# One 88-entry phase table for the S5 scan in a two-layer hybrid inference kernel

## The chip, the cores and the metric

The kernel runs on one core of a Trainium2 chip. The metric is the device time of one execution in microseconds (us). Three timed runs of the kernel before are given, and one more execution was taken with the profiler; every row of the trace is from that one.

## The reference, cut to what matters

The program is one inference step of a two-layer backbone with 128 context tokens and 512 latent tokens, 640 in all. Each layer has three token mixers (differential attention, gated linear attention called GLA, and a bidirectional S5 state-space scan), a gated merge, an output projection and a SwiGLU feed-forward network (FFN). The change concerns the S5 scan alone:

```python
def s5_scan(u, lam_re, lam_im, log_dt, b_re, b_im, c_re, c_im, h0, reverse):
    dt = jnp.exp(log_dt)[:, None]
    mag = jnp.exp(lr * dt)
    ar = mag * jnp.cos(li * dt)
    ai = mag * jnp.sin(li * dt)
...
    pr, pim, hr, hi = lax.associative_scan(complex_affine_combine, (a_r, a_i, bu_r, bu_i), axis=1, reverse=reverse)
    hr = pr * h0r - pim * h0i + hr
    hi = pr * h0i + pim * h0r + hi
    y = einsum('gip,blgp->blgi', c_re, hr) - einsum('gip,blgp->blgi', c_im, hi)
```

It runs forward and backward over 32 channel groups of 16 channels, with 64 complex states per group.

## The kernel before

**The S5 scan.** Tokens are taken in chunks of 8, which gives 16 context chunks, 64 latent chunks and a gap column. The first 64 partitions hold the states of the forward direction and the other 64 those of the backward direction. Eight blocks e of four groups each are worked one after the other. Within a block, `s5_pre` projects the input into the chunk states dS (82 columns per group), turns each column back by the phase of its chunk (function `rot`, lines 818 to 821), runs a real-valued decaying scan on VectorE, and turns the columns forward again with a second `rot`. The phases come from a table PH of 2 x 4 x 82 numbers per partition.

**The tables.** `s5_tables` makes, for one layer, what these blocks need: powers PA of the decay, powers E1 (0 to 8) and E8 of the phase of a chunk, and then per block a row buffer R that holds the projection W (1024 numbers), PH and the output table Vc (1280 numbers). R is written out to DRAM as R_d by a DMA on GpSimd's queue (L447), and a second small result Z as Z_d (L459). `s5_load` later reads W and PH back (L779, L780). R has two buffers. The scratch tile tp_ of the phase product has one buffer, and that is the buffer of Z: the first product into tp_ of a block waits until Z_d of the block before has been written. `cmul` (lines 334 to 340) is a complex product of six VectorE instructions, two of which write the scratch.

**PH before.** The two directions have their latent segment at different columns, so each half of the partitions gets a product of its own: 64 entries at column 17 for the forward half, at column 0 for the backward half. ScalarE then copies the 65th entry from a tile E64 (L479) and copies the first 17 entries into the context segment (L480). That is twelve VectorE instructions of 64 partitions x 256 elements and eight ScalarE copies per block.

**Order.** [...] The tables of layer 0 are built at the start of the program, between the modulation, the first norm, the input projection of the S5 branch and the first gate projections. `GLA_FILL` lists which table blocks (T) and gate projections (e) are written where; all of layer 0's blocks are done before the GLA mixer opens. The tables of layer 1 are built inside layer 0's FFN, one block at each "t" of `FFN_FILL`. Every dense projection needs VectorE too: the weights are split into a high part whi on ScalarE (L90) and a low part wlo on VectorE (L201) before TensorE multiplies (L232).

Of the kernel before, what the change touches and what calls it, by code (L numbers as in the profile page):

```python
# [10 lines left out]
F32 = mybir.dt.float32  # L11
# [4 lines left out]
ALU = mybir.AluOpType  # L16
# [4 lines left out]
P = 128  # L21
# [23 lines left out]
    a="AAAAAAAA",  # L45
    s="AAAAAAADAAAAAAADAAAAAAAAAAADADAAAAAAAADADAADAAAAAAAAADAAAAAAAAAADADAAAAAADAADAAAAAAAAADAAA"
       "AAAAAAAADADAAAAAADDDAAAAAAAAAAADAAAAADDAAAAAAAAAAAAAAA",
    r="AADAAAADAAAAAADADAAADAAAAADAAAAADAAADAAAAADAADAD",
# [5 lines left out]
    g="AAAAAAAADAAAAAAA")  # L54
# [8 lines left out]
EPS = 1e-6  # L63
NCH = T // 8
SP_ = 82
RV = 1024 + 8 * SP_
RW = RV + 1280
VEC = dict(n1g=(0, 8), n2g=(8, 8), bmod=(16, 48), qn=(64, 1), kn=(65, 1), sub=(66, 1),
           on=(67, 1), ba=(68, 4), s5d=(72, 4), bglu=(76, 8))
# [7 lines left out]
def tile_hybrid(ctx: ExitStack, tc: tile.TileContext, i: dict, o: dict):  # L77
# [264 lines left out]
    def s5_tables(l, tb, tabs):  # L342
# [54 lines left out]
        for _ in range(3):  # L397
            dve.tensor_mul(t1, co, co)
            dve.tensor_mul(t2, si, si)
            dve.tensor_mul(si, co, si)  # L400
            dve.tensor_scalar_mul(si, si, 2.0)
            dve.tensor_sub(co, t1, t2)
        def bc(ap, n):
            return ap.to_broadcast([P, 32, n])

# [7 lines left out]
        def powers(name, n, r, i_):  # L413
            X = tb.tile([P, 2, 32, n], F32, tag=name, name=f"{name}_{l}", bufs=1)
            pool.memset(X[:, 0, :, 0:1], 1.0)
            pool.memset(X[:, 1, :, 0:1], 0.0)
            dve.tensor_copy(X[:, 0, :, 1], r)
            dve.tensor_copy(X[:, 1, :, 1], i_)
            double(X, 1)
            double(X, 2)  # L420
            double(X, 4, min(4, n - 5))
            return X

        PA = powers("PA", 9, Ar, Ai)
        E1 = powers("E1", 9, co, si)
        E8 = powers("E8", 8, E1[:, 0, :, 8], E1[:, 1, :, 8])
        E64 = tb.tile([P, 2, 32], F32, tag="E64", name=f"E64_{l}", bufs=1)
        cmul(E64[:, 0], E64[:, 1], E8[:, 0, :, 7], E8[:, 1, :, 7], E8[:, 0, :, 1], E8[:, 1, :, 1], tt[:, :, 0], dve, dve)
        PP = tb.tile([P, 2, 32, 10], F32, tag="PP", name=f"PP_{l}", bufs=1)
        pool.memset(PP, 0.0)  # L430
        PW = tb.tile([P, 2, 32, 8], F32, tag="PW", name=f"PW_{l}", bufs=1)
# [29 lines left out]
        for e in range(8):  # L461
            gs = slice(e * 4, e * 4 + 4)
            R = tb.tile([P, RW], F32, tag="R", name=f"R{l}_{e}", bufs=2)
            PH = R[:, 1024:RV].rearrange("p (a b c) -> p a b c", a=2, b=4)
            Vc = R[:, RV:].rearrange("p (g r x o) -> p g r x o", g=4, r=2, o=16)
            tp_ = tb.tile([P, 4, 8, 8], F32, tag="Z", name=f"tp{l}_{e}", bufs=1)
            for rows, w0, w1 in ((slice(0, 64), 17, 0), (slice(64, P), 0, 65)):
                def o64(j):
                    return PH[rows, j, :, w0:w0 + 64].rearrange("p g (a b) -> p g a b", a=8)

                def e1(j):
                    return E1[rows, j, gs, 0:8].unsqueeze(2).to_broadcast([64, 4, 8, 8])

                def e8(j):
                    return E8[rows, j, gs].unsqueeze(3).to_broadcast([64, 4, 8, 8])

                cmul(o64(0), o64(1), e8(0), e8(1), e1(0), e1(1), tp_[rows], dve, dve)
                for j in range(2):
                    act.copy(PH[rows, j, :, w0 + 64:w0 + 65], E64[rows, j, gs].unsqueeze(2))  # L479
                    act.copy(PH[rows, j, :, w1:w1 + 17], PH[rows, j, :, w0:w0 + 17])  # L480
            bcr = bc8[:, e]
            FBt = tb.tile([P, 2, 4, 32], F32, tag="FB", name=f"FB{l}_{e}", bufs=2)
            pool.memset(FBt[:, :, :, 16:32], 0.0)
            FB = FBt[:, :, :, 0:16]
            tm = tb.tile([P, 4, 10, 16], F32, tag="tm", name=f"tm{l}_{e}", bufs=2)
            tf = tm[:, :, 0, :]

            def fb(j):
                return f[:, j * 32 + e * 4:j * 32 + e * 4 + 4].unsqueeze(2).to_broadcast([P, 4, 16])

            cmul(FB[:, 0], FB[:, 1], bcr[:, 0], bcr[:, 1], fb(0), fb(1), tf, dve, dve)
            Wc = tb.tile([P, 4, 2, 8, 16], F32, tag="Wc", name=f"Wc{l}_{e}", bufs=2)

            def pw(t, n):
                return t.unsqueeze(3).to_broadcast([P, 4, n, 16])

            def mid(t, n):
                return t.unsqueeze(2).to_broadcast([P, 4, n, 16])

            cmul(Wc[:, :, 0], Wc[:, :, 1], pw(PW[:, 0, gs], 8), pw(PW[:, 1, gs], 8),  # L500
                 mid(FB[:, 0], 8), mid(FB[:, 1], 8), tm[:, :, 0:8], dve, dve)
            cr, ci = mid(bcr[:, 2], 10), mid(bcr[:, 3], 10)
            tv = tb.tile([P, 4, 10, 16], F32, tag="tm", name=f"tv{l}_{e}", bufs=2)
            dve.tensor_mul(Vc[:, :, 0], cr, pw(PP[:, 0, gs], 10))
            dve.tensor_mul(tv, ci, pw(PP[:, 1, gs], 10))
            dve.tensor_sub(Vc[:, :, 0], Vc[:, :, 0], tv)
            dve.tensor_mul(Vc[:, :, 1], cr, pw(PP[:, 1, gs], 10))
            dve.tensor_mul(tv, ci, pw(PP[:, 0, gs], 10))
            v1 = Vc[:, :, 1].rearrange("p g x o -> p g (x o)")
            dve.scalar_tensor_tensor(v1, v1, -1.0, tv.rearrange("p g x o -> p g (x o)"), op0=ALU.mult, op1=ALU.subtract)  # L510
            cur = (e, R, Wc, FBt, Vc)
            if l == 0:
                tail(*cur)
            elif e:
                tail(*pend)
            pend = cur
            yield
# [256 lines left out]
    subg_of = {}  # L774

    def s5_load(l, e, spa, tabs):
        PH = spa.tile([P, 2, 4, SP_], F32, tag="s_PH", name=f"PH{l}_{e}", bufs=2)
        W = spa.tile([P, 4, 2, P], F32, tag="s_W", name=f"W{l}_{e}", bufs=2)
        sync.dma_start(W.rearrange("p a b c -> p (a b c)"), tabs[0][e, :, 0:1024])  # L779
        sync.dma_start(PH.rearrange("p a b c -> p (a b c)"), tabs[0][e, :, 1024:RV])  # L780
        return W, PH

# [7 lines left out]
    def s5_pre(l, e, sp, r8, RM, ut, s0, fs):  # L790
        gs = slice(e * 4, e * 4 + 4)
        u = ut[e // 4][:, (e % 4) * 4:(e % 4) * 4 + 4, :]
        W, PH = RM

        def tU(role, name, bufs=2):
            return sp.tile([P, 2, 4, SP_], F32, tag="s_" + role, name=f"{name}{l}_{e}", bufs=bufs)

        DEC = sp.tile([P, 4, SP_], F32, tag="s_DEC", name=f"DEC{l}_{e}", bufs=2)
        dve.tensor_mul(DEC, dmask.unsqueeze(1).to_broadcast([P, 4, SP_]),
                        r8[:, e * 4:e * 4 + 4].unsqueeze(2).to_broadcast([P, 4, SP_]))  # L800
        pd = ps_m(f"pds{l}_{e}")
        for g in range(4):
            for ri in range(2):
                pe.matmul(pd[:, ri, g * 81:(g + 1) * 81], W[:, g, ri, :], u[:, g, :], start=True, stop=True)  # L804
        pdv = pd[:, :, 0:324].rearrange("p r (g n) -> p r g n", g=4)
        dS = tU("dS", "dS")
        copy("D", "A", dS[0:64, :, :, 1:17], pdv[0:64, :, :, 0:16])
        copy("D", "A", dS[0:64, :, :, 18:82], pdv[0:64, :, :, 17:81])
        copy("D", "A", dS[64:P, :, :, 81:65:-1], pdv[64:P, :, :, 0:16])
        copy("D", "A", dS[64:P, :, :, 64:0:-1], pdv[64:P, :, :, 17:81])  # L810
        pool.memset(dS[0:64, :, :, 0:1], 0.0)
        pool.memset(dS[64:P, :, :, 65:66], 0.0)
        pool.tensor_copy(dS[0:64, :, :, 17:18], s0[0:64, :, gs].unsqueeze(3))
        pool.tensor_copy(dS[64:P, :, :, 0:1], s0[64:P, :, gs].unsqueeze(3))
        P1, P2, H = tU("P1", "P1", 1), tU("P2", "P2", 1), tU("H", "H")

        def rot():
            fv = "p r g n -> p r (g n)"
            for j, Pj in ((0, P1), (1, P2)):
                dve.tensor_mul(Pj.rearrange(fv), dS.rearrange(fv),  # L820
                               PH[:, j:j + 1].rearrange(fv).to_broadcast([P, 2, 4 * SP_]))

        rot()
        dve.tensor_add(P1[:, 0], P1[:, 0], P2[:, 1])
        dve.tensor_sub(P1[:, 1], P1[:, 1], P2[:, 0])
        fl = "p g n -> p (g n)"
        for ri in range(2):
            dve.tensor_tensor_scan(dS[:, ri].rearrange(fl), DEC.rearrange(fl), P1[:, ri].rearrange(fl), 0.0, ALU.mult, ALU.add)
        rot()
        lo, hi = slice(0, 64), slice(64, P)  # L830
        for ri, op in ((0, dve.tensor_sub), (1, dve.tensor_add)):
            op(H[lo, ri], P1[lo, ri], P2[lo, 1 - ri])
            op(H[hi, ri, :, 80::-1], P1[hi, ri, :, 0:81], P2[hi, 1 - ri, :, 0:81])
            op(fs[hi, ri, gs].unsqueeze(2), P1[hi, ri, :, 81:82], P2[hi, 1 - ri, :, 81:82])
        pool.tensor_copy(fs[lo, :, gs].unsqueeze(3), H[lo, :, :, 16:17])
        return u, H
# [554 lines left out]
```

## Time and profile before

| | |
|---|---|
| timed runs | 2743.64, 2752.35, 2761.11 us (median 2752.35) |
| profiled execution | 2768.95 us |
| its span, first to last instruction | 2767.2 us |
| mean granted TensorE clock | 0.957 of full speed |
| TensorE, VectorE, ScalarE busy | 2608.2, 1683.7, 869.3 us |

Busy times are of the whole span. The tables take a small part of it, in two stretches: about 10 to 180 us (layer 0) and about 990 to 1395 us (layer 1). In the profile DVE is VectorE, ACT is ScalarE, PE is TensorE, POOL is GpSimd and SP the queue that issues loads.

### The profile page before, as it was taken

How to read it: one execution, taken by the hardware profiler on the slowest of the kernel's cores; microseconds unless marked ns; L12 is line 12 of the kernel's file. 1: busy time of each engine (PE TensorE's matmuls, PEld its weight loads, DVE VectorE, ACT ScalarE, POOL GpSimd, SP SyncE). 2: the span in 40 equal slices, each digit the busy share in tenths (PEclk: the TensorE clock that was granted, in tenths of full speed). 3: DMA queues.
4: the chain of work that ended last, by engine and by line, in shares of the span. 5: the costliest groups of instructions: out<-in, count | busy, mean ns of one | idle time of the engine just before them, and what ended most of it. 6: DMA issues, size and time to landing. Idle time of an engine off the chain costs nothing.

```text
span 2767.2 us, 45251 instructions
## 1 busy us (share of the span) xinstructions
PE 2608.2 (94%) x18528; PEld 2445.5 (88%) x18528; DVE 1683.7 (61%) x3784; ACT 869.3 (31%) x1617; POOL 71.6 (3%) x194
## 2 busy tenths in 40 slices
PE   5859989999999999989999799999999999999999
PEld 3748869988999989879999698899999999999999
DVE  8956567856644687677346626695764456434443
ACT  4424322245332431221214424322543233121211
POOL 0110000000000000000000000010000000000000
PEclk8979998989999999999999799999999999999999
DMA  7444344521122334454443123253211241222222
GB/s 264 152 156 128 107 147 126 148 78 43 48 62 85 111 126 139 151 182 144 161 144 105 43 80 79 91 158 99 69 48 55 76 134 45 75 77 77 77 74 79
DMA packets 123918, 293.45 MB, mean 106 GB/s; under 512 B 36256, under 2 KB 59808, under 8 KB 121664
## 3 DMA queue, kind: packets, MB, share of 16 engines
q1 hardware_dynamic: 116672, 248.59, 28.6%
q0 software_dynamic: 7040, 41.98, 4.1%
q8 instruction: 146, 2.39, 0.4%
q14 instruction: 60, 0.49, 0.1%
HBM read 252.12 MB, written 42.60 MB: 107 GB/s over the span
## 4 chain that ended last, share of the span: by engine, by line
PE 72%; DVE 15%; DMA 5%; ACT 4%; issue 3%; SPq 0%; POOL 0%; ACTq 0%; DVEq 0%; POOLq 0%
PE pd L232 59%; DVE wlo L201 2%; ACT whi L90 2%; PE pa L638 2%; PE ps L733 2%; PE pw L763 1%; PE py L845 1%; PE pmod L172 1%; PE po L667 1%; PE pw L757 1%; DMA raw<-in_w_down_dram 1%; DMA wm<-in_w_mod_dram 1%; DMA Z_d<-Z 1%; PE pds L804 1%; PE po L664 1%
## 5 line engine op out<-in xcount | busy, mean ns | idle before, releaser
L201 DVE TENSOR_TENSOR wlo<-raw,whi 128x1024 fp32r<-128x1024 f32 (+1 forms) x306 | 352.6, 1154 | 413.0 <-ACT whi L90 412.1
L90 ACT CAST whi<-raw 128x1024 fp32r<-128x1024 f32 (+1 forms) x273 | 270.8, 993 | 723.7 <-PE pd L232 596.8
L232 PE MATMUL pd<-hh0a,whi 128*128 128x320 f32 x848 | 280.0, 331 | 9.1 <-ACT mg__3_516 L880 3.1
L232 PE MATMUL pd<-hh0a,wlo 128*128 128x320 f32 x848 | 275.0, 324 | 1.3 <-DVE wlo L201 1.2
L232 PE MATMUL pd<-hh1a,whi 128*128 128x320 f32 x848 | 265.1, 313 | 9.4 <-ACT mg__1_514 L880 5.2
L232 PE MATMUL pd<-hl0a,whi 128*128 128x320 f32 x848 | 272.4, 321 | 0.8 <-DVE hl0a L325 0.8
L232 PE MATMUL pd<-hl1a,whi 128*128 128x320 f32 x848 | 264.7, 313 | 0.0
L232 PE MATMUL pd<-hh1a,wlo 128*128 128x320 f32 x848 | 264.0, 312 | 0.0
L232 PE MATMUL pd<-ah,whi 128*128 128x320 f32 x704 | 222.2, 316 | 7.9 <-DVE ft L1157 1.6
L232 PE MATMUL pd<-hh0b,whi 128*128 128x320 f32 x704 | 220.1, 313 | 4.7 <-DVE ft L1154 3.2
L232 PE MATMUL pd<-al,whi 128*128 128x320 f32 x704 | 219.0, 311 | 0.5 <-DVE al L201 0.5
L232 PE MATMUL pd<-ah,wlo 128*128 128x320 f32 x704 | 219.2, 312 | 0.2 <-DVE wlo L201 0.2
L232 PE MATMUL pd<-hh1b,whi 128*128 128x320 f32 x704 | 218.0, 310 | 1.1 <-DVE ft L1154 1.1
L232 PE MATMUL pd<-hh0b,wlo 128*128 128x320 f32 x704 | 218.6, 311 | 0.0
L232 PE MATMUL pd<-hl0b,whi 128*128 128x320 f32 x704 | 218.4, 310 | 0.0
L232 PE MATMUL pd<-hl1b,whi 128*128 128x320 f32 x704 | 217.7, 309 | 0.0
L232 PE MATMUL pd<-hh1b,wlo 128*128 128x320 f32 x704 | 217.7, 309 | 0.0
L232 PEld LDWEIGHTS pd<-hh0a,whi 128*128 128x128 f32 x848 | 168.6, 199 | 16.9 <-issue 6.2
L232 PEld LDWEIGHTS pd<-hh0a,wlo 128*128 128x128 f32 x848 | 167.7, 198 | 6.2 <-DVE wlo L201 3.2
L232 PEld LDWEIGHTS pd<-hh1a,whi 128*128 128x128 f32 x848 | 160.9, 190 | 11.9 <-ACT mg__1_514 L880 5.8
L232 PEld LDWEIGHTS pd<-hl0a,whi 128*128 128x128 f32 x848 | 168.2, 198 | 2.4 <-DVE hl0a L325 1.4
L232 PEld LDWEIGHTS pd<-hl1a,whi 128*128 128x128 f32 x848 | 160.8, 190 | 0.5 <-DVE hl1a L325 0.3
(502 smaller groups left out, 5769.5 us busy)
## 6 DMA issues: line engine op xcount, KB each, us to landing
raw<-in_w_in_dram SPq DMA_DIRECT2D x104, 512.0 KB, 3.9
wm<-in_w_mod_dram SPq DMA_DIRECT2D x96, 512.0 KB, 4.3
R_d<-R POOLq DMA_DIRECT2D x16, 1480.0 KB, 6.4
raw<-in_w_gate_dram SPq DMA_DIRECT2D x44, 512.0 KB, 3.5
raw<-in_w_up_dram SPq DMA_DIRECT2D x44, 512.0 KB, 3.5
raw<-in_w_down_dram SPq DMA_DIRECT2D x40, 512.0 KB, 3.5
raw<-in_w_branch_dram SPq DMA_DIRECT2D x24, 512.0 KB, 3.5
W<-R_d SPq DMA_DIRECT2D x16, 512.0 KB, 3.6
```

The lines of the kernel that those rows point to most:

```text
L90: (e.copy if e is act else e.tensor_copy)(dst, src)
L172: pe.matmul(pm[cg * 32:(cg + 1) * 32, 0:256], scond[:, kc, :], wt[:, cg, :], start=(kc == k0), stop=(kc == k0 + per - 1), tile_position=(0 ...
L201: dve.tensor_sub(lo, src, hi.bitcast(F32))
L232: pe.matmul(ps[:, :HT], ww, xx[hf][:, kc, :], start=(n == 0 and j == 0), stop=(n == last and j == 2))
L638: pe.matmul(pa[:, r, n * P:(n + 1) * P], km[r * 64:r * 64 + 64, t * P:(t + 1) * P], qm[r * 64:r * 64 + 64, t * P:(t + 1) * P], start=True, ...
L664: pe.matmul(dst, vt[:, t, hd * P:(hd + 1) * P], at[:, t, hd, :], start=True, stop=(t == 0))
L667: pe.matmul(dst, S[rows, d, t, :], qE[rows, d, ts_], start=False, stop=(d == 1))
L733: pe.matmul(pS[:, bank, off:off + n], qn[rows, q0:q0 + P], src[rows, a:a + n], start=True, stop=True)
L757: pe.transpose(pw[:, t * P:(t + 1) * P], E[0][:, t * P:(t + 1) * P], ident)
L763: pe.matmul(po, vv, WT[:, t * P:(t + 1) * P], start=(t == 0), stop=(t == nk // P - 1))
L804: pe.matmul(pd[:, ri, g * 81:(g + 1) * 81], W[:, g, ri, :], u[:, g, :], start=True, stop=True)
L845: mm = pe.matmul(dst, Vt[:, 2 * g + ri, :], H[:, ri, g, 0:81], start=False, stop=(ri == 1))
```

## The change

The phase of a column only matters relative to the other columns of its segment. So the table becomes one running product, phase to the power n for n = 0 to 87, the same for every segment and both directions. It is made by one `cmul` over all 128 partitions with 352 elements (11 x 8 per group); the two half-partition products, E64 and the ScalarE copies go. Since the powers now run further, the phase is scaled to length one before its powers and once more after the eighth (function `unit`, five VectorE instructions each), and E8 has 11 entries in place of 8. PH grows from 82 to 88 columns, in R, in R_d and in the tile that `s5_load` fills; `rot` reads the first 82 of them, so its operands are no longer flattened over the groups.

```diff
-RV = 1024 + 8 * SP_
+SQ_ = 88
+RV = 1024 + 8 * SQ_
...
+        def unit(z):
+            dve.tensor_mul(t1, z[:, 0], z[:, 0])
+            dve.tensor_mul(t2, z[:, 1], z[:, 1])
+            dve.tensor_add(t1, t1, t2)
+            dve.tensor_scalar(t1, t1, -0.5, 1.5, op0=ALU.mult, op1=ALU.add)
+            dve.tensor_mul(z, z, t1.unsqueeze(1).to_broadcast([P, 2, 32]))
+
+        unit(cs.rearrange("p (c g) -> p c g", c=2))
...
             double(X, 4, min(4, n - 5))
+            if n > 9:
+                double(X, 8, n - 9)
...
-        E8 = powers("E8", 8, E1[:, 0, :, 8], E1[:, 1, :, 8])
-        E64 = tb.tile([P, 2, 32], F32, tag="E64", name=f"E64_{l}", bufs=1)
-        cmul(E64[:, 0], E64[:, 1], E8[:, 0, :, 7], E8[:, 1, :, 7], E8[:, 0, :, 1], E8[:, 1, :, 1], tt[:, :, 0], dve, dve)
+        unit(E1[:, :, :, 8])
+        E8 = powers("E8", 11, E1[:, 0, :, 8], E1[:, 1, :, 8])
...
-            tp_ = tb.tile([P, 4, 8, 8], F32, tag="Z", name=f"tp{l}_{e}", bufs=1)
-            for rows, w0, w1 in ((slice(0, 64), 17, 0), (slice(64, P), 0, 65)):
-                def o64(j):
-                    return PH[rows, j, :, w0:w0 + 64].rearrange("p g (a b) -> p g a b", a=8)
-
-                def e1(j):
-                    return E1[rows, j, gs, 0:8].unsqueeze(2).to_broadcast([64, 4, 8, 8])
-
-                def e8(j):
-                    return E8[rows, j, gs].unsqueeze(3).to_broadcast([64, 4, 8, 8])
-
-                cmul(o64(0), o64(1), e8(0), e8(1), e1(0), e1(1), tp_[rows], dve, dve)
-                for j in range(2):
-                    act.copy(PH[rows, j, :, w0 + 64:w0 + 65], E64[rows, j, gs].unsqueeze(2))
-                    act.copy(PH[rows, j, :, w1:w1 + 17], PH[rows, j, :, w0:w0 + 17])
+            tp_ = tb.tile([P, 4, 11, 8], F32, tag="Z", name=f"tp{l}_{e}", bufs=1)
+
+            def ph(j):
+                return PH[:, j].rearrange("p g (a b) -> p g a b", a=11)
...
+            cmul(ph(0), ph(1), e8(0), e8(1), e1(0), e1(1), tp_, dve, dve)
...
-        PH = spa.tile([P, 2, 4, SP_], F32, tag="s_PH", name=f"PH{l}_{e}", bufs=2)
+        PH = spa.tile([P, 2, 4, SQ_], F32, tag="s_PH", name=f"PH{l}_{e}", bufs=2)
...
-            fv = "p r g n -> p r (g n)"
             for j, Pj in ((0, P1), (1, P2)):
-                dve.tensor_mul(Pj.rearrange(fv), dS.rearrange(fv),
-                               PH[:, j:j + 1].rearrange(fv).to_broadcast([P, 2, 4 * SP_]))
+                dve.tensor_mul(Pj, dS, PH[:, j:j + 1, :, 0:SP_].to_broadcast([P, 2, 4, SP_]))
```

## Rows read from the trace of the kernel before

**Rows 1.** The page: span, and busy time of two engines with their instructions.

```profile
span 2767.2 us, 45251 instructions
PE 2608.2 (94%) x18528; PEld 2445.5 (88%) x18528; DVE 1683.7 (61%) x3784; ACT 869.3 (31%) x1617; POOL 71.6 (3%) x194
```

**Rows 2.** Stretches of layer 0's tables: length, busy time by engine, PE clock.

```profile
16.00:35.00 19.00, 13.20 (x131) 4.91 (x133) 18.58 (x100) 5.97 (x20) 0.00 (x0) 0.87 1.01 380
75.00:100.00 25.00, 24.43 (x145) 23.87 (x146) 22.64 (x47) 13.39 (x29) 4.11 (x5) 0.87 0.49 116
100.00:120.00 20.00, 18.30 (x182) 17.29 (x181) 19.68 (x48) 8.12 (x21) 2.60 (x6) 1.00 0.48 167
120.00:140.00 20.00, 14.81 (x110) 12.69 (x110) 16.71 (x35) 4.83 (x14) 1.29 (x3) 0.91 0.46 169
140.00:180.00 40.00, 13.35 (x127) 8.09 (x128) 37.58 (x79) 9.81 (x31) 2.90 (x6) 0.53 0.24 92
```

**Rows 3.** Groups of VectorE instructions by shape, 0 to 185 us.

```profile
L336 DVE TENSOR_TENSOR tp<-E,E 64x256 f32<-64x256 f32 x16 | 6.7, 418 | 4.7 <-DMA Z_d<-Z 4.5
L504 DVE TENSOR_TENSOR R<-bc,PP 128x640 f32<-128x640 f32 x8 | 6.6, 821 | 0.0
...
L335 DVE TENSOR_TENSOR Wc<-PW,FB 128x512 f32<-128x512 f32 x8 | 5.5, 687 | 0.0
...
L398 DVE TENSOR_TENSOR t<-cs 128x32 f32<-128x32 f32 x3 | 0.5, 182 | 0.0
L401 DVE TENSOR_SCALAR cs<-cs 128x32 f32<-128x32 f32 x3 | 0.5, 175 | 0.0
...
L335 DVE TENSOR_TENSOR E<-E 128x64 f32<-128x64 f32 x2 | 0.5, 242 | 0.0
```

**Rows 4.** VectorE's instructions in order of time, two parts of 155 to 180 us.

```profile
162.19 0.41 DVE L335 TENSOR_TENSOR R<-E,E 64x256 f32<-64x256 f32 x1
162.52 0.81 DVE L510 SCALAR_TENSOR_TENSOR R<-R,tv 128x640 f32<-128x640 f32 x1
...
171.31 0.87 DVE L336 TENSOR_TENSOR tp<-E,E 64x256 f32<-64x256 f32 x2
...
174.91 0.69 DVE L340 TENSOR_TENSOR Wc<-Wc,tm 128x512 f32<-128x512 f32 x1
...
176.25 1.22 DVE L201 TENSOR_TENSOR wlo<-raw,whi 128x1024 fp32r<-128x1024 f32 x1
```

**Rows 5.** Groups of ScalarE instructions by shape, 16 to 200 us.

```profile
L480 ACT COPY R<-R 64x68 f32<-64x68 f32 x32 | 8.0, 249 | 22.4 <-DVE R L337 14.5 <-DVE R L340 7.6
L479 ACT COPY R<-E 64x4 f32<-64x4 f32 x32 | 5.1, 193 | 28.4 <-DMA R_d<-R 23.0 <-DVE E L337 5.1
```

**Rows 6.** Instructions in order of time, 131 to 143 us.

```profile
131.37 0.54 POOL L459 DMA_DIRECT2D Z_d<-Z  x1
...
140.80 0.59 ACT L479 COPY R<-E 64x4 f32<-64x4 f32 x4 [6.11 <-DMA R_d<-R]
141.05 0.87 DVE L336 TENSOR_TENSOR tp<-E,E 64x256 f32<-64x256 f32 x2 [4.07 <-DMA Z_d<-Z]
...
142.84 0.63 PE L232 MATMUL pd<-hh1a,whi 128*128 128x320 f32 x1 [5.00 <-ACT mg__1_514 L880]
```

**Rows 7.** Tile Z: the times of its DMAs to landing.

```profile
DMA to landing us min/median/max: 2.0/4.4/9.7
```

**Rows 8.** Stretches of layer 1's tables, columns as in Rows 2.

```profile
1000.00:1050.00 50.00, 47.87 (x343) 44.39 (x343) 49.08 (x142) 18.01 (x41) 0.00 (x0) 1.00 0.49 161
1150.00:1200.00 50.00, 45.59 (x354) 41.13 (x353) 42.16 (x93) 10.50 (x31) 2.55 (x6) 0.97 0.54 192
1200.00:1250.00 50.00, 43.90 (x373) 39.72 (x372) 39.73 (x85) 13.29 (x38) 2.78 (x7) 0.93 0.44 161
```

**Rows 9.** Tile PH: the rotation's line, and its loads' times to landing.

```profile
L820 DVE TENSOR_TENSOR P<-dS,PH x64: 824/836/847, 437.0 to 1877.6; 128x656 f32<-128x656 f32 x64
...
DMA to landing us min/median/max: 2.8/4.2/7.4
```

More of the change, by code (lines that the diff above doesn't have):

```diff
@@ L465, in s5_tables, with e1, e8 @@
             Vc = R[:, RV:].rearrange("p (g r x o) -> p g r x o", g=4, r=2, o=16)
-            tp_ = tb.tile([P, 4, 8, 8], F32, tag="Z", name=f"tp{l}_{e}", bufs=1)
-            for rows, w0, w1 in ((slice(0, 64), 17, 0), (slice(64, P), 0, 65)):
-                def o64(j):
-                    return PH[rows, j, :, w0:w0 + 64].rearrange("p g (a b) -> p g a b", a=8)
-                def e1(j):
-                    return E1[rows, j, gs, 0:8].unsqueeze(2).to_broadcast([64, 4, 8, 8])
-                def e8(j):
-                    return E8[rows, j, gs].unsqueeze(3).to_broadcast([64, 4, 8, 8])
-                cmul(o64(0), o64(1), e8(0), e8(1), e1(0), e1(1), tp_[rows], dve, dve)
-                for j in range(2):
-                    act.copy(PH[rows, j, :, w0 + 64:w0 + 65], E64[rows, j, gs].unsqueeze(2))
-                    act.copy(PH[rows, j, :, w1:w1 + 17], PH[rows, j, :, w0:w0 + 17])
+            tp_ = tb.tile([P, 4, 11, 8], F32, tag="Z", name=f"tp{l}_{e}", bufs=1)
+            def ph(j):
+                return PH[:, j].rearrange("p g (a b) -> p g a b", a=11)
+            def e1(j):
+                return E1[:, j, gs, 0:8].unsqueeze(2).to_broadcast([P, 4, 11, 8])
+            def e8(j):
+                return E8[:, j, gs].unsqueeze(3).to_broadcast([P, 4, 11, 8])
+            cmul(ph(0), ph(1), e8(0), e8(1), e1(0), e1(1), tp_, dve, dve)
             bcr = bc8[:, e]
```

## The prediction

> **What bounds the kernel now.** I read the page first: TensorE is busy 2608.2 of 2767.2 us [rows 1], so a cut on VectorE or ScalarE counts only where TensorE is short of work. The second view is the busy time by stretch over the two places where tables are built. In layer 0, from 140 to 180 us, VectorE is busy 37.58 of 40 us and TensorE 13.35 [rows 2]: the program waits for VectorE there. From 75 to 120 us both are nearly full, VectorE with 42.3 and TensorE with 42.7 of 45 us, so that 2.3 us at most can be won for TensorE. From 16 to 35 us VectorE has 18.58 of 19 us [rows 2]. The order of time says why TensorE starves late: blocks of the table follow each other on VectorE without a weight split in between, until wlo at 176.25 us [rows 4], and no gate projection can start without its wlo. In layer 1 the tables lie in the FFN; VectorE is full from 1000 to 1050 us (49.08 of 50), but TensorE still has 47.87, 45.59 and 43.90 of 50 us in the three stretches shown, so 12.6 us of its idle time is all that there is to win in them [rows 8].
>
> **The blocks' product.** Twelve instructions of 64x256 at 418 ns are 5.02 us per block [rows 3]. The new six are 128x352, a shape that the trace lacks. Between 64x256 (418) and 128x512 (687) one element costs (687 - 418) / 256 = 1.05 ns, and the number of partitions shows no price of its own: 640 elements on the same line give 821 [rows 3]. So 352 elements cost 418 + 96 x 1.05 = 519 ns, and six cost 3.11 us. That saves 1.91 us per block. The bounds come from starts: eight of the old instructions fill 171.31 to 174.91 us, 450 ns each, while one that stands before an unrelated instruction lets that start after 0.33 us though it lasts 0.41 [rows 4]. With 32 ns more or 80 ns less on each new one, six cost 3.3 or 2.6 us, and a block saves 1.7 to 2.4 us. I take 1.91, since both kernels have both kinds of neighbours. Eight blocks of a layer save 15.3 us of VectorE's work.
>
> [...]
>
> **The setup of each layer.** A call of unit is three products or sums of 32 elements (182 ns), a scale (175) and one of 64 elements (242): 0.96 us, and there are two [rows 3]. E8's third doubling grows by 32 elements, 6 x 34 ns = 0.2 us; a fourth with 64 elements costs 6 x 242 ns = 1.45 us; E64's product goes, 6 x 182 ns = 1.1 us. That adds 2.5 us, or about 1.7 us if the ten additional instructions overlap by the 80 ns seen above [rows 4]. It lies where VectorE is full [rows 2], so in layer 0 it counts in whole; in layer 1 it precedes the full stretch [rows 8] and takes its part of the gain there.
>
> **Where layer 0's saving lands.** A block is 31 VectorE instructions (12 of the product, 6 for FB, 6 for Wc, 6 for Vc, 1 for Z). From 120 to 180 us VectorE runs 35 + 79 = 114 [rows 2]; less a few for weight splits, that is 3.5 blocks. They pass in full, 3.5 x 1.91 = 6.7 us, because wlo stands behind them. Two blocks lie ahead of 75 us: 3.8 us less the setup's 2.5 leave 1.3 us, which I count whole. The 2.5 blocks from 75 to 120 us save 4.8 us, of which I count the 2.3 us that TensorE idles. Together 10.3 us; the ends are 4.2 us (the late blocks less the setup, nothing else) and 12.8 us (all of it).
>
> **The scratch's wait.** tp_ still shares its one buffer with Z. Once VectorE waited 4.07 us for Z_d [rows 6], of 4.5 us in all in this layer [rows 3]. Of the work that may stand ahead of the first scratch product, 4 x 418 shrinks to 2 x 519 ns, so 0.6 us of cover goes; I charge it at one block, 0.6 us. Z_d takes 2.0 to 9.7 us to land, 4.4 in the middle [rows 7].
>
> **ScalarE's copies.** 32 of 249 ns and 32 of 193 ns go in layer 0, 14.1 us of work, and with them 23.0 us in which these copies stood at the head of ScalarE's queue until R_d had freed the buffer of R [rows 5]. Behind one of them the gate's eviction waited, and TensorE lost 5.00 us for it [rows 6]. ScalarE's next write to R is then the copy of W, which comes late in the block. I count nothing, as TensorE would have run dry before wlo at 176.25 us all the same [rows 4]; at most it is those 5 us. The wait for the buffer of R itself moves to VectorE's first write, which stands after the whole block before it; I take 0 there, and at most 4 us, the size of the wait that VectorE did have for Z_d [rows 6].
>
> **Rotation, loads, writes.** The rotation keeps its 656 elements; only the form of its operands changes. A product with a broadcast over four dimensions takes 821 ns for 640 [rows 3], which scales to 838 for 656, and the flat one takes 836 [rows 9]: 0, within 64 x 10 ns = 0.6 us either way. PH's load grows by 88/82, and 4.2 us to landing [rows 9] become 4.5. It is issued two blocks ahead on SP's queue: 0, at most 16 x 0.3 = 5 us if no block hid it. R_d grows by 1.6% and is waited for by no engine on the path: 0, below 0.2 us per block (1.6% of the 9.4 us from Z_d's issue to the copies' start in [rows 6]).
>
> **Layer 1.** 15.3 less 2.5 is 12.8 us less for VectorE, and more than 14 us less for ScalarE. TensorE's 12.6 us of idle time [rows 8] have other causes too, the evictions and the loads. I take 3 us, between 0 and 6.
>
> **The sum.** 10.3 - 0.6 + 3 = 12.7 us less. From the profiled execution, 2768.95 us (span 2767.2), that gives 2756.2. The median of the timed runs lies 16.6 us below the profiled execution, and none of the stretches named is known to be shorter in it, so I subtract the same 12.7 us there: **2739.6**, say 2740.
>
> **Rivals.** (a) TensorE or a load holds everything before 120 us, and the FFN hides layer 1. Then 4.2 us remain: 2748. For it: both engines are full from 75 to 120 us [rows 2]. Against it: an earlier end of a block also lets the next block start earlier. (b) The freed ScalarE queue counts as well: 12.8 + 5 in layer 0 and 6 in layer 1, 23.8 us: 2728.5. For it: the 23.0 us of waits and the 5.00 us of TensorE [rows 5, 6]. Against it: wlo decides. (c) Slower: the scratch becomes the bound. All six instructions now depend on one scratch, and the block that precedes it is shorter. If VectorE waits at each of layer 0's seven boundaries as it did at one, that is 7 x 4.07 = 28.5 us, 24.4 more than now; less the gain of 12.7 it makes 11.7 us more: 2764. It decides as soon as the additional wait is above 1.9 us per block. For it: 9.7 us to landing at worst [rows 7]. Against it: seven of eight blocks hardly waited. [...]
>
> **How the numbers follow.** Chances: forecast 0.50 (its own range 2732 to 2747), (a) 0.20, (b) 0.15, (c) 0.08, (d) 0.07. The three runs scatter by 9 us around their median. The range reaches from (b) less 6 us of scatter to (a) with 9 us on top: 2722 to 2757; (c) and part of (d) lie outside. One per cent, about what a measurement of this kernel can tell from no change, is 27.5 us; no case alone reaches it. Faster by more needs (b) with every bound at its best: 0.08. Slower by more needs (c) with more than the seven waits: 0.03. Within: 0.89.
>
> **What would show it.** Right: six products of 128x352 at about 519 ns per block and no copies at the two ScalarE lines; the last block of layer 0 ends near 167 us where it ended near 178 now, and the FFN's tables hardly move the end. Wrong: a product above 560 ns; VectorE idle until Z_d or R_d at most blocks; a rotation above 850 ns; TensorE as dry as before between 120 and 170 us.

## The result and the profile after

| | before | after |
|---|---|---|
| median of the timed runs | 2751.34 us (4 runs, 2743.64 to 2761.11) | 2720.69 us (4 runs, 2717.81 to 2724.87) |
| profiled span | 2767.2 us | 2716.0 us |
| mean granted TensorE clock | 0.957 | 0.968 |

The ratio is 0.9891, 95% interval 0.9864 to 0.9918: some 31 us less, where 12.7 us were forecast; the median lies 1.3 us below 2722, the lower end of the range. A second profile of the kernel before (experiment 4) has a span of 2745.7 us at a clock of 0.966, so 21 us of the 51 us between the two spans above are not the change's. Where it matters, both profiles of before are used below, and two of after (a repeat is among the experiments).

The page after, its head, which answers to [rows 1]; the product's and two other groups by shape from 0 to 185 us, for [rows 3]:

```profile
span 2716.0 us, 45049 instructions
...
PE 2585.1 (95%) x18528; PEld 2427.3 (89%) x18528; DVE 1652.2 (61%) x3708; ACT 843.5 (31%) x1489; POOL 71.5 (3%) x194
```

```profile
L513 DVE TENSOR_TENSOR tv<-bc,PP 128x640 f32<-128x640 f32 x8 | 6.6, 824 | 0.0
...
L336 DVE TENSOR_TENSOR Wc<-PW,FB 128x512 f32<-128x512 f32 x8 | 5.5, 690 | 0.0
L337 DVE TENSOR_TENSOR tp<-E,E 128x352 f32<-128x352 f32 x8 | 4.2, 523 | 0.2 <-DMA Z_d<-Z 0.2
```

A product instruction lasts 523 ns, near the forecast (519). The wait for Z_d is 0.2 us where it was 4.5 [rows 3]. VectorE in order of time, after, for [rows 4]:

```profile
130.51 0.52 DVE L336 TENSOR_TENSOR R<-E,E 128x352 f32<-128x352 f32 x1
130.95 0.52 DVE L337 TENSOR_TENSOR tp<-E,E 128x352 f32<-128x352 f32 x1
131.38 0.52 DVE L339 TENSOR_TENSOR R<-E,E 128x352 f32<-128x352 f32 x1
131.82 0.52 DVE L338 TENSOR_TENSOR R<-R,tp 128x352 f32<-128x352 f32 x1
132.25 0.69 DVE L338 TENSOR_TENSOR Wc<-Wc,tm 128x512 f32<-128x512 f32 x1
```

The reader is to look at the first column, not the second: each starts 0.435 us after the one before, so six take 2.61 us of VectorE's time. In the kernel before, the same view shows both kinds of distance:

```profile
113.84 0.86 DVE L336 TENSOR_TENSOR tp<-E,E 64x256 f32<-64x256 f32 x2
114.73 0.88 DVE L337 TENSOR_TENSOR R<-R,tp 64x256 f32<-64x256 f32 x2
...
117.44 0.42 DVE L335 TENSOR_TENSOR R<-E,E 64x256 f32<-64x256 f32 x1
117.78 0.41 DVE L338 TENSOR_TENSOR R<-E,E 64x256 f32<-64x256 f32 x1
```

An "x2" row is the same product on the two halves of the partitions, one after the other: 0.45 us each. Two products that I take for the same half are 0.34 us apart; the view doesn't name the half, and experiment 11 is the test of this reading. Over layer 0's stage the mean distance is 0.422 us before (92 starts with no idle time behind them) and 0.443 us after (46 starts): 12 x 0.422 - 6 x 0.443 = 2.4 us per block. In the late blocks, where the pairs stand together, it is 5.13 us (eight distances of 0.45, four of 0.33 to 0.43) less 2.61, 2.5 us. By durations it was 1.91.

Now the whole stage. When the fourth and the last block of layer 0 were sent off (R_d on GpSimd's queue), before and after:

```profile
117.99 0.54 POOL L447 DMA_DIRECT2D R_d<-R  x1 [3.74 <-ACT R L480]
...
178.76 0.54 POOL L447 DMA_DIRECT2D R_d<-R  x1 [12.02 <-ACT R L90]
```

```profile
113.37 0.54 POOL L458 DMA_DIRECT2D R_d<-R  x1 [3.14 <-ACT Z L468]
...
156.03 0.54 POOL L458 DMA_DIRECT2D R_d<-R  x1 [8.96 <-issue]
```

The last block, forecast near 167 us, is sent off at 156.03. The stretch between the two, and then the rows that answer to [rows 2]; columns as there. Before, then after:

```profile
117.99:178.76 60.77, 27.23 (x229) 19.96 (x235) 55.59 (x118) 14.72 (x45) 4.74 (x11) 0.68 0.31 118
```

```profile
113.37:156.03 42.66, 26.70 (x240) 22.16 (x241) 42.00 (x86) 7.72 (x15) 4.72 (x10) 0.74 0.50 190
...
120.00:140.00 20.00, 12.34 (x124) 10.47 (x130) 19.98 (x44) 5.64 (x11) 2.36 (x5) 0.84 0.44 177
140.00:180.00 40.00, 28.63 (x215) 25.57 (x205) 18.01 (x31) 6.33 (x14) 7.15 (x12) 0.78 0.65 226
```

The four late blocks take 18.1 us less. VectorE is busy 13.6 us less in them (32 instructions fewer: 24 of the products, 8 that now fall outside), and its idle time falls from 5.18 to 0.66 us, the scratch's wait. VectorE remains the bound there: 42.00 of 42.66 us. TensorE, 13.35 us busy from 140 to 180 us before, is busy 28.63 us there after. The first GLA read, the end of this stage, in the kernel before and after:

```profile
L622 DVE TENSOR_TENSOR X<-bcrc x14: 484/490/493, 229.2 to 385.8; 128x320 f32<-128x320 f32 x14
```

```profile
L630 DVE TENSOR_TENSOR X<-bcrc x14: 481/488/497, 203.0 to 359.7; 128x320 f32<-128x320 f32 x14
```

It begins 26.2 us earlier. [Rows 5] have no answer, since the copies are gone; for [rows 7] and [rows 9] the profile shows no surprise, Z's DMA and the rotation:

```profile
DMA to landing us min/median/max: 2.0/4.7/8.9
...
L827 DVE TENSOR_TENSOR P<-dS,PH x64: 821/835/844, 409.5 to 1831.4; 128x656 f32<-128x656 f32 x64
```

This table goes through all profiles (us). The first column is the start of the first read above; the second the first read of layer 0's FFN gate, tile ft, less that; the third the time from the first to the last read of ft in layer 0, in which layer 1's tables are built (reads by VectorE's SCALAR_TENSOR_TENSOR ft<-ft,pd); the fourth the rest up to the end of the span.

| kernel | to GLA | to FFN | FFN, layer 0 | rest | span |
|---|---|---|---|---|---|
| before | 229.2 | 731.0 | 505.2 | 1301.8 | 2767.2 |
| before again (4) | 228.7 | 724.2 | 504.2 | 1288.6 | 2745.7 |
| after | 203.0 | 721.3 | 498.4 | 1293.3 | 2716.0 |
| after again (12) | 201.0 | 723.0 | 499.5 | 1293.7 | 2717.2 |
| two products of 256 (1) | 216.2 | 721.6 | 487.4 | 1296.4 | 2721.6 |
| copies back (2) | 199.5 | 729.6 | 496.6 | 1296.9 | 2722.6 |
| layer 0 only (3) | 201.0 | 718.5 | 506.9 | 1291.0 | 2717.4 |
| before, own scratch (5) | 223.9 | 718.0 | 490.1 | 1296.0 | 2728.0 |
| no unit (6) | 200.0 | 729.4 | 485.7 | 1295.8 | 2710.9 |
| before, 88 columns (7) | 225.4 | 726.3 | 507.0 | 1293.9 | 2752.6 |
| before, copies on GpSimd (8) | 228.2 | 722.7 | 507.5 | 1294.5 | 2752.9 |
| after, own scratch (9) | 201.2 | 726.3 | 485.7 | 1298.5 | 2711.7 |
| after, pair apart (10) | 199.6 | 724.1 | 488.8 | 1288.7 | 2701.2 |
| before, one half (11) | 214.5 | 723.8 | 488.0 | 1299.5 | 2725.8 |

Two columns carry the differences: the first (27.0 us between the means of the two pairs) and the third (5.8 us). The second and fourth move by 13 us over all kernels, and by 7 and 13 us between the two profiles of before: scatter.

### The profile page after: what moved, and what is told of

It reads as the page before. It is cut to its first block, busy times and chain, and to the rows that moved or that the text cites. A ratio compares the mean times of both kernels' runs of the same rounds, so it can differ in the third digit from the quotient of the medians.

```text
span 2716.0 us, 45049 instructions
## 1 busy us (share of the span) xinstructions
PE 2585.1 (95%) x18528; PEld 2427.3 (89%) x18528; DVE 1652.2 (61%) x3708; ACT 843.5 (31%) x1489; POOL 71.5 (3%) x194
## 4 chain that ended last, share of the span: by engine, by line
PE 77%; DVE 13%; ACT 4%; DMA 4%; issue 2%; SPq 0%; ACTq 0%; DVEq 0%
PE pd L233 64%; DVE wlo L202 2%; PE ps L741 2%; PE pa L646 2%; ACT whi L91 2%; PE pw L771 1%; PE pmod L173 1%; PE py L851 1%; DMA raw<-in_w_up_dram 1%; PE po L675 1%; DMA wm<-in_w_mod_dram 1%; PE pw L765 1%; PE pds L812 1%; PE po L672 1%; PE pq L265 1%
```

## The experiments

Each ratio is to the kernel before, timed beside the variant (its medians: 2752.5 to 2754.1 us).

**1. Two products of 256 elements on all partitions.** The new table, made as entries 0 to 63 and 24 to 87.

```diff
-            cmul(ph(0), ph(1), e8(0), e8(1), e1(0), e1(1), tp_, dve, dve)
+            for a0 in (0, 3):
+                def ph(j):
+                    return PH[:, j, :, a0 * 8:a0 * 8 + 64].rearrange("p g (a b) -> p g a b", a=8)
...
+                cmul(ph(0), ph(1), e8(0), e8(1), e1(0), e1(1), tp_, dve, dve)
```

> The phase product is made by twelve instructions of 128x256 per block (columns 0 to 63, then 24 to 87, so that some columns are computed twice), the same number and size as before the change, but on all 128 partitions; the copies stay away. Theory H (an instruction on half of the partitions next to one that starts on another half cannot overlap with it): the twelve start 0.34 us after each other and take 4.0 us per block against 5.1 before and 2.6 after; the last block of layer 0 is written out near 167 us and the time is about 2734. Theory D (the price is the profiled duration, as in the prediction, and the additional gain has another cause): the twelve take 5.0 us per block, the last block comes near 175 us, the time is about 2742. Theory A (the gain beyond the prediction comes from ScalarE's copies): starts as in D, but the time keeps 15 us or more of the gain over the kernel before.

Measured: 2722.81 us, ratio 0.9886 (0.9871 to 0.9901). VectorE in order of time:

```profile
143.27 0.42 DVE L336 TENSOR_TENSOR R<-E,E 128x256 f32<-128x256 f32 x1
143.61 0.42 DVE L339 TENSOR_TENSOR R<-E,E 128x256 f32<-128x256 f32 x1
143.94 0.42 DVE L337 TENSOR_TENSOR tp<-E,E 128x256 f32<-128x256 f32 x1
144.28 0.22 DVE L340 TENSOR_TENSOR tm<-bc,f 128x64 f32<-128x64 f32 x1
```

The duration is that of the 64-partition product, the distance 0.335 us and not 0.45; the mean of 92 starts is 0.343 us, 4.1 us per block. The last block was sent off at 174.94 us, where theory H said 167 and D 175, because the wait for Z_d grew to 7.2 us here. Set beside the kernel after, eight blocks by starts (11.7 us) and the wait (6.9) come to 18.6 us, and the last block is 18.8 us later than in its two profiles: theory H's price holds, and the wait is why its 167 was missed. The time lies 11 us below H's 2734, as the third column made up for the rest, which no theory had foreseen then.

Six of the 92 distances are above 0.4 us, and five of them have a cause of their own:

```profile
170.36 0.42 DVE L337 TENSOR_TENSOR tp<-E,E 128x256 f32<-128x256 f32 x1
170.81 0.43 DVE L338 TENSOR_TENSOR R<-R,tp 128x256 f32<-128x256 f32 x1
171.27 0.42 DVE L340 TENSOR_TENSOR tp<-E,E 128x256 f32<-128x256 f32 x1
171.61 0.42 DVE L336 TENSOR_TENSOR R<-E,E 128x256 f32<-128x256 f32 x1
```

The second instruction reads the scratch that the first has just written, and the third writes it again: 0.45 and 0.46 us, with all 128 partitions. The fourth touches no scratch and starts 0.34 us behind the third. In the kernel after, the three such starts are 0.56 us apart (from 153.31 us on).

**2. ScalarE's copies back.** The new table and eight copies per block that ScalarE makes as before.

```diff
+            for rows in (slice(0, 64), slice(64, P)):
+                for j in range(2):
+                    act.copy(PH[rows, j, :, 87:88], E8[rows, j, gs, 10:11])
+                    act.copy(PH[rows, j, :, 0:17], PH[rows, j, :, 0:17])
```

> The kernel after with ScalarE's eight copies per block put back, in the same forms (64x4 out of the table of powers into column 87, 64x68 of columns 0 to 16 onto themselves), so that ScalarE has the old work and the old waits for R's buffer. Theory H: VectorE decides in this stretch, the last block of layer 0 is written out at 156 to 160 us and the time stays within 5 us of 2721. Theory A (the copies and their waits at the head of ScalarE's queue cost the time): 10 to 20 us slower than the kernel after, with the last block near 170 us.

Measured: 2722.65 us, ratio 0.9876 (0.9857 to 0.9896); the last block was sent off at 159.36 us and the GLA read came at 199.5. The theory that the gain comes from ScalarE's queue falls.

**3. The new table in layer 0 only.** Layer 1 keeps the old products, E64 and copies.

```diff
+            if l == 0:
+                cmul(ph(0), ph(1), e8(0), e8(1), e1(0), e1(1), tp_, dve, dve)
+            else:
+                for rows, w0, w1 in ((slice(0, 64), 17, 0), (slice(64, P), 0, 65)):
...
```

> The new table product and setup in layer 0 only; layer 1 keeps the two half products, E64 and the copies, and fills the six additional columns with zeros on GpSimd. Theory: layer 0's stretch carries 26 us of the gain and layer 1's 5, so about 2726 us. Rival (both layers gain the same amount, and the span of one profile misleads): about 2736.

Measured: 2732.2 us (6 runs, 2719.15 to 2741.8), ratio 0.9923 (0.9907 to 0.994). The median lies between the theory's 2726 and the rival's 2736 and decides for neither; the profile is of the fastest of the six. By its columns, the first is that of after (201.0), the third that of before (506.9). So layer 0's new tables give the 27 us of the first column, and layer 1's the 7.4 to 8.5 us by which the third column is shorter in the whole change (498.4 and 499.5).

**4. The kernel before again**, unchanged, for its profile.

> The kernel before without an edit, for a second profile. The spans of the first profiles differ by 51 us and the medians by 31. Theory: the difference of 20 us is TensorE's granted clock in the S5 and attention stages, which varies from one execution to the next; a second profile has its last block of layer 0 again near 179 us, the wait for Z_d near 4 us again or not, and a span of 2735 to 2770. Rival: the 20 us belong to the change (the S5 stages of both layers are shorter after it): the second profile then shows 200 us again for 430 to 630.

Measured: 2747.47 us. Its last block of layer 0 was sent off at 178.45 us (178.76), the wait for Z_d was 4.4 us (4.5): layer 0 repeats to 0.5 us. The second and fourth columns are 7 and 13 us shorter than in the first profile of the same kernel; the granted clock is 0.966 over the span where it was 0.957, and 0.94 from 430 to 630 us where it was 0.89. So these 20 us are not the change's; that the clock is their cause was not shown.

**5. The kernel before with a scratch of its own.**

```diff
-            tp_ = tb.tile([P, 4, 8, 8], F32, tag="Z", name=f"tp{l}_{e}", bufs=1)
+            tp_ = tb.tile([P, 4, 8, 8], F32, tag="tp", name=f"tp{l}_{e}", bufs=1)
```

> The kernel before with a buffer of its own for the product's scratch, so that it no longer waits until Z_d is written. Theory W (the waits of 4.5 us in layer 0 were on the path, one part of the gain that the prediction gave the wrong sign): the last block is written out near 174.5 us in place of 178.5 and the time falls by about 4 us, to 2747. Rival (something else is late at that place): the last block at 178 us and no change.

Measured: 2730.44 us (8 runs, 2727.27 to 2747.0), ratio 0.9927 (0.9901 to 0.9953). The wait for Z_d is gone, and 5 us of the first column. The last block was sent off at 172.12 us, 2.4 us before the expected 174.5, for the products' mean distance fell as well, from 0.422 to 0.398 us: 2.3 us over 96 starts, which I put down to another order of the halves. The time fell by 20 us, which was not expected: the third column fell by 14 us. The edit had changed the order of layer 1's blocks in the queues: R_d of two blocks had been sent off 6.6 us apart, now no two are nearer than 18.3 us.

**6. No scaling to length one.** The new table without the two calls of unit.

```diff
-        unit(cs.rearrange("p (c g) -> p c g", c=2))
...
-        unit(E1[:, :, :, 8])
```

> The kernel after without the two calls of unit in each layer; it leaves out the scaling of the phase to length one. Theory (VectorE is full in layer 0's setup, ten instructions at about 0.17 us from start to start): 1.7 us less in the stretch up to the GLA stage, about 2719 us. Rival (the setup is covered by the loads of the modulation weights): no change, 2721 us.

Measured: 2707.89 us, ratio 0.9826 (0.9785 to 0.9867), 13 us less than after. In layer 0 the second block was sent off at 67.34 us (68.18), and from the third (102.39, against 102.12) nothing of the saving is left. Both expectations (2719 and 2721) missed the total. The third column is again the one that fell, to 485.7 us.

**7. Only the 88 columns and the rotation's new form**, on the kernel before (W, PH and R_d as long as after).

```diff
-                dve.tensor_mul(Pj.rearrange(fv), dS.rearrange(fv),
-                               PH[:, j:j + 1].rearrange(fv).to_broadcast([P, 2, 4 * SP_]))
+                dve.tensor_mul(Pj, dS, PH[:, j:j + 1, :, 0:SP_].to_broadcast([P, 2, 4, SP_]))
```

> The kernel before with only the 88-column table, its larger row, write and load, and the rotation in its new form; the half products, E64 and the copies stay, and GpSimd fills the six additional columns with zeros. Theory (as in the prediction, this part costs nothing): rotation at 836 ns, time within 4 us of the kernel before. Rival (the larger transfers or the strided rotation cost something that the table's gain hid): 5 us or more slower.

Measured: 2753.87 us, ratio 1.0 (0.998 to 1.002); the rotation takes 835 ns. It costs nothing in the time; the first column is 3.5 us shorter, as the wait for Z_d fell to 0.3 us here.

**8. The copies on GpSimd**, on the kernel before.

```diff
-                    act.copy(PH[rows, j, :, w1:w1 + 17], PH[rows, j, :, w0:w0 + 17])
+                    pool.tensor_copy(PH[rows, j, :, w1:w1 + 17], PH[rows, j, :, w0:w0 + 17])
```

> The kernel before with the eight copies per block moved from ScalarE to GpSimd, so that ScalarE's queue is freed of their work and their waits and VectorE keeps its twelve half products. Theory H (VectorE decides): the last block stays at 174 to 179 us and the time within 5 us of the kernel before. Theory A (ScalarE's queue held TensorE back): 10 us or more of the gain appears here, 2741 or less.

Measured: 2757.03 us, ratio 1.0009 (0.9981 to 1.0036). ScalarE freed of all 64 copies of a layer changes nothing; together with experiment 2 this settles it from both sides.

**9. The new table with a scratch of its own**, the edit of experiment 5 on the kernel after.

> The new table with a scratch buffer of its own, no longer that of Z. Theory O (the 20 us that the own scratch gave the kernel before were only 5 us of waiting in layer 0; the rest came from another order of layer 1's blocks in the queues): VectorE waits only 0.2 us for Z_d in the changed kernel, so the first GLA read stays at 203 us, but the queue order is of the better kind here too, and the first FFN stretch, from the first to the last read of ft in layer 0, falls from 498 to 486 to 490 us: 2709 to 2713 us in all. Rival: the gain of the own scratch was the wait for Z_d itself, in both layers; then there is almost nothing left to win: 2717 to 2722 us.

Measured: 2715.76 us (2713.43 to 2720.98), ratio 0.9874 (0.9827 to 0.9921). The third column did as theory O says, 485.7 us; the first did not move (201.2). Of those 13 us only some 3 reached the end, beside 2718.84 of experiment 12, and the 2709 to 2713 us expected were missed: the second and fourth columns are 3 to 5 us longer. What lengthens them stays open; it is within their scatter.

**10. The pair apart.** The kernel after with one letter moved.

```diff
-FFN_FILL = ".mm.mm.mo..mt.mtmm..mt.mtmmmttmm.....mmm.tm.m.mmttttmttmtmtm"
+FFN_FILL = ".mm.mm.mo..mt.mtmm..mt.mtmmmtmtm.....mmm.tm.m.mmttttmttmtmtm"
```

> The changed kernel with one letter of FFN_FILL moved, so that the sixth block of layer 1 is written one weight step later than the fifth, not right behind it. Nothing of layer 0 changes: first GLA read at 203 us. Theory O: in the changed kernel two blocks end 4.5 us apart near 1185 us, TensorE loses 6.5 of 25 us there and the granted clock falls to 0.88; with the pair apart some 6 to 10 us of that come back: 2711 to 2716 us. Rival (that idle time is due to the evictions and the loads, whatever stands where): 2718 to 2723 us.

Measured: **2706.93 us** (2703.0 to 2713.3), ratio 0.9838 (0.9797 to 0.9879), the fastest of the kernels with the whole computation, 4 us below the range expected. Busy time where the pair stood, in the kernel after and then with the pair apart (columns as in [rows 8]):

```profile
1175.00:1200.00 25.00, 18.09 (x186) 15.86 (x185) 21.21 (x49) 4.56 (x10) 2.58 (x6) 0.97 0.45 167
1200.00:1225.00 25.00, 25.00 (x164) 24.22 (x165) 21.80 (x47) 5.19 (x8) 0.54 (x1) 0.89 0.45 162
```

```profile
1175.00:1200.00 25.00, 24.55 (x213) 22.54 (x212) 24.19 (x53) 5.08 (x11) 1.83 (x4) 1.00 0.50 172
1200.00:1225.00 25.00, 25.00 (x173) 24.93 (x172) 16.86 (x32) 6.26 (x10) 0.00 (x0) 1.00 0.36 115
```

TensorE loses 6.91 us in the first 25 us with the pair, 0.45 us without, and the granted clock of the two stretches is 0.97 and 0.89 with it, 1.00 and 1.00 without. In the repeat of the kernel after (12) TensorE loses 5.01 us there, and the clock is 0.93 and 0.93. The blocks' times on GpSimd's queue, with the pair and without:

```profile
1183.11 0.53 POOL L458 DMA_DIRECT2D R_d<-R  x1 [7.08 <-ACT R L91]
1187.61 0.53 POOL L458 DMA_DIRECT2D R_d<-R  x1 [0.51 <-PE pk L463]
```

```profile
1192.03 0.53 POOL L458 DMA_DIRECT2D R_d<-R  x1 [14.93 <-ACT R L91]
...
1278.31 0.53 POOL L458 DMA_DIRECT2D R_d<-R  x1 [1.23 <-ACT R L91]
```

The sixth block went further than one step: it is now sent off at 1278.31 us, 90 us later, so the run shows what a stretch with one block less is worth, not what a small distance is. Two blocks 4.5 us apart keep VectorE's queue from the gate's products and weight splits that TensorE waits for (4.0 and 0.7 us of its waits from 1170 to 1205 us in the kernel after); theory O holds. VectorE's own work is only part of it; in the kernel after it also waits there:

```profile
1195.47 0.70 DVE L91 CAST whi<-raw 128x1024 fp32r<-128x1024 f32 x1 [3.65 <-DMA raw<-in_w_up_dram]
```

That load was issued at 1188.02 us, 0.06 us after the weight split wlo of 1186.74 us had ended, which stood behind the work of the pair; 4.0 of TensorE's 6.91 us end with products behind this wait.

The other profiles agree: in the six where no two blocks of layer 1 are sent off less than 8.8 us apart, the third column is 485.7 to 490.1 us; in the eight where two are 4.5 to 6.6 us apart it is 496.6 to 507.5.

**11. Both halves on the same partitions.** The kernel before, with the backward product also on partitions 0 to 63, into a tile and with a scratch of its own.

```diff
-                    return E1[rows, j, gs, 0:8].unsqueeze(2).to_broadcast([64, 4, 8, 8])
+                    return E1[lo, j, gs, 0:8].unsqueeze(2).to_broadcast([64, 4, 8, 8])
...
-                cmul(o64(0), o64(1), e8(0), e8(1), e1(0), e1(1), tp_[rows], dve, dve)
+                cmul(o64(0), o64(1), e8(0), e8(1), e1(0), e1(1), tp_[lo] if w0 else t2_, dve, dve)
```

> The kernel before with its two products of 64 partitions both computed on partitions 0 to 63 (the backward half of the table is left zero, its product goes to a spare tile). Same count, same shape, same arithmetic per instruction; only the alternation between the two halves of the partitions goes. Theory H (an instruction on the other half of the partitions doesn't start until the one before has ended): starts 0.33 us apart in place of 0.45, the product 4.0 to 4.2 us per block in place of 5.1, the last block of layer 0 is issued near 169 to 172 us in place of 178.5 (the shared scratch is split here, so that some of the 4 us wait for Z_d may go as well). Rival (64 partitions are slow as such, or the chain through the scratch makes the distance): starts stay at 0.45 us and the last block is issued near 174 to 178 us.

Measured: 2727.79 us in one run. VectorE in order of time:

```profile
151.38 0.41 DVE L338 TENSOR_TENSOR R<-E,E 64x256 f32<-64x256 f32 x1
151.71 0.41 DVE L335 TENSOR_TENSOR o<-E,E 64x256 f32<-64x256 f32 x1
152.05 0.41 DVE L336 TENSOR_TENSOR t<-E,E 64x256 f32<-64x256 f32 x1
152.38 0.21 DVE L335 TENSOR_TENSOR FB<-bc,f 128x64 f32<-128x64 f32 x1
...
153.30 0.41 DVE L339 TENSOR_TENSOR t<-E,E 64x256 f32<-64x256 f32 x1
153.63 0.21 DVE L336 TENSOR_TENSOR tm<-bc,f 128x64 f32<-128x64 f32 x1
```

The distance is 0.33 to 0.34 us in 91 of 93 starts, mean 0.337 (before: 0.422). The order of the instructions changed with the edit, so the three products in a row at the head of the fence are the ones to compare with the pairs before. The same shape with the same arithmetic is 0.12 us cheaper than at a change of halves, as soon as the instruction beside it starts at the same partition. The last block was sent off at 165.79 us. That is 3 us before the range given, since the wait for Z_d went as well: 96 starts at 0.085 us less and 4.5 us of wait are 12.6 us, and it came 12.8 us earlier than before.

**12. The kernel after again**, beside 9 and 10.

> The changed kernel once more, beside the two above on the same chip. Both theories: 2717 to 2725 us, first GLA read at 203 us, first FFN stretch 498 us. If these stage times move by more than 3 us without any edit, the 7 to 12 us that theory O reads from that stretch can't be told from scatter.

Measured: 2718.84 us (2716.87 to 2724.57), ratio 0.9882 (0.9842 to 0.9923). The first column moved by 2.0 us, the third by 1.1: what theory O reads from the third column, 7 to 14 us, stands above that.

## Why the prediction was wrong

Layer 0 was put at 10.3 us less the scratch's 0.6, 9.7 in all; it gave 27.0. By the prediction's own steps, the 17.3 us between them are: the scratch's wait 4.9, the stretch behind the last block 4.5, the product's price 3.9, the setup 1.5, and the saving that was not let through 2.5. Three steps failed above all: the product was priced by durations, the scratch's wait was put at a loss without a reason, and the stretch behind the last block was not in the sum.

**The scratch's wait: wrong sign.** I charged 0.6 us more; it fell by 4.3, from 4.5 to 0.2 us. Experiments 1 (7.2 us) and 7 (0.3 us) show that it comes and goes, and with ScalarE's copies back (2) the new table has 3.3 us of it again. So this part of the gain is not the product's doing but luck; that the order of the queue decides it is argued, not shown. Experiment 5 takes the wait away: the last block comes 6.5 us earlier, against 4.5 for the wait and 2.3 for the shorter distances there. I had excluded a gain without a reason.

**The product's price.** "Twelve instructions of 64x256 at 418 ns are 5.02 us per block", six new ones 3.11, 1.91 us saved. The new duration was right to 4 ns. But the last block's time followed the starts, and the two kinds of instruction differ in how far the next one overlaps them: over the stage the old ones last 0.418 us and start 0.422 us apart, the new ones last 0.523 and start 0.443 us apart. A block saves 2.4 us over the stage and 2.5 in the late blocks, at and above the upper bound; eight blocks save 19.2 us, not 15.3. The rows with 450 and 330 ns were in front of me [rows 4]; I took them for bounds ("both kernels have both kinds of neighbours"), varied the six new instructions by them, left the twelve old ones at 418 ns, and did not ask what the slow pairs share. Experiments 1 and 11 show it: a change from one half of the partitions to the other, 0.45 us from start to start against 0.33. Without such changes a block would save 12 x 0.335 - 6 x 0.435 = 1.41 us, by the distances of experiments 1 and 11 and of the kernel after. The other 1.0 us is the alternation.

**Where layer 0's saving lands.** To the fourth block 4.4 us came (4.6 and 4.1 in the two pairs of profiles), near the 1.3 and 2.3 us that I counted for that part. Behind it I had 6.7 us, and the four blocks became 18.1 us shorter: 10.1 from the products by starts, 4.1 from the wait above, and as a remainder 3.9 from other instructions of the blocks that now stand on the other side of a block's end. The cap by TensorE's idle time from 75 to 120 us did not bind: VectorE's queue handed what was saved on to the late blocks. All fourteen profiles bear this out: take the products of layer 0 by starts (their number times the mean distance where VectorE doesn't idle) and the wait for Z_d from the time at which the last block is sent off, and 132.4 to 135.0 us are left in each, while that time itself goes from 153.41 to 178.76 us. Nothing in the sum stood for the last 4.5 us, which lie behind the last block (from 50.3 to 45.8 us up to the GLA read). The stretch before, then after (columns as in [rows 2]):

```profile
178.00:229.00 51.00, 47.79 (x325) 44.90 (x325) 15.12 (x24) 17.54 (x28) 6.07 (x10) 0.94 0.53 171
```

```profile
156.00:203.00 47.00, 43.83 (x299) 41.65 (x298) 13.91 (x22) 16.96 (x27) 6.07 (x10) 0.98 0.53 169
```

TensorE has some 25 matmuls fewer to do there, since they were done earlier (the whole program has the same 18528), and a granted clock of 0.98 where it was 0.94. How the 4.5 us divide between the two was not told apart.

**ScalarE's copies, rotation, loads, setup.** The copies are worth nothing (experiments 2 and 8), the columns and the rotation nothing (7): right. The setup was put at 2.5 us and counted whole; the rest named above is 1.0 us longer in the two profiles of after than in the two of before, and experiment 6 shows 0.8 us for the two calls of unit at the second block, and none from the third on.

**Layer 1.** 3 us (0 to 6) were forecast, 5.8 us came in the third column, 7.4 to 8.5 beside experiment 3. The term was too small by 3 to 5 us, and what it left out is where the blocks stand in the queues: a scratch's tag took 14 us off the same stretch, and one letter 10 us. Among the profiles without a close pair of blocks, the old products have 488.0 and 490.1 us (11, 5) and the new ones 485.7 to 488.8 (6, 9, 10), so the saved work by itself shows as 4.4 us at most. How the change's 5.8 us divide between work and order was not told apart.

**The rivals.** (a) and (c) did not occur. (b) gave a size (23.8 us) closer to the measured one from a cause that experiments 2 and 8 exclude. (d) stood for a shift of the work in the stages behind, 8 us to either side by my estimate; no run shows that figure. What the runs show is larger: where the order of layer 1's blocks differs, the FFN's stretch moves by up to 14 us (experiment 5). Its part in this change is open: the kernel before has two pairs of neighbouring blocks there (6.6 and 7.7 us apart), the kernel after one (4.5 us), and 5.8 us lie between them.

**The level.** Subtracting from the median and not from the one profiled execution was right: the two stages give 27.0 + 5.8 = 32.8 us by the profiles, the medians 30.7, and the other 18 us between the two first spans don't repeat in experiment 4.

## What to carry to other kernels

Price VectorE's instructions by the distance of their starts in the timeline, not by their duration (2.4 us saved per block here against 1.91), and where two distances occur for one shape, find what the slow pairs share before taking a mean; pairs that alternate between halves of the partitions (0.45 us here against 0.34) are the first thing to look for, and an instruction that needs what the one before it has just written (0.45 against 0.34 in experiment 1) is the second. In the stage that VectorE bounds here, what was saved on it reached the stage's end to within 2.6 us in all fourteen profiles, whatever the other engines were doing in its middle. After any edit to work that is spread as filler, look where the pieces now stand in the queues of the later stages: moving one of two that stood side by side was worth another 12 us here (2706.93 against 2718.84), 10 of them in the stretch where they stand.

## What the runs showed of the hardware that was not expected

A 64x256 product lasts 0.40 to 0.43 us wherever it stands, but the next start comes 0.33 us later if the neighbour begins at the same partition and 0.45 us later if it begins at the other half (experiment 11 and the kernel before); on 128 partitions it is 0.335 us in a row of such products (experiment 1), and 0.45 us there when it needs the scratch that the one before has just written. From 128x256 to 128x352 the distance grows by 0.100 us, 1.04 ns per element; by the line through the two, an estimate, 0.07 us per instruction are paid for by no element. And behind 6.91 us of TensorE's idle time, the granted clock was 0.89 of full speed on the mean of the next 25 us, and 0.93 behind 5.01 us in the repeat (experiment 12); behind 0.45 us, in experiment 10, it was 1.00.
